# Summing and listing the presence of experts over 82 blocks instead of 128

## The chip, the core and the metric

The kernel runs on one core of a Trainium2 chip. The metric is the device time of one execution, in microseconds. TensorE (PE; its weight loads PEld) multiplies matrices into PSUM; VectorE (DVE), ScalarE (ACT) and GpSimd (POOL) work beside it; SyncE (SP) issues most DMAs, and GpSimd the indirect ones.

## The reference

A trunk of two layers on 256 frames of 1024 channels: latent attention, then sparse attention, each followed by PEER, a mixer that picks 16 of 16384 experts for each of 8 heads of a token. The change touches PEER alone:

```python
v1, i1 = lax.top_k(s1, PEER_TOPK)
v2, i2 = lax.top_k(s2, PEER_TOPK)
...
best, pos = lax.top_k(cand, PEER_TOPK)
expert = jnp.take_along_axis(cand_idx, pos, axis=-1)
gate = jax.nn.softmax(best, axis=-1)
...
    u = w_down[e_blk]
    a = jnp.einsum('td,ted->te', x_blk, u).astype(jnp.float32)
    hg = (jax.nn.gelu(a, approximate=False) * g_blk).astype(w_up.dtype)
    return jnp.einsum('te,ted->td', hg, w_up[e_blk]).astype(x_blk.dtype)
```

So each token uses 128 experts: a row of `w_down`, a gelu, a gate, and a row of `w_up`.

## The kernel before

**Blocks.** The 16384 experts form 128 blocks of 128. For the down projection the kernel doesn't gather: for each block it multiplies all 128 rows of `w_down` with all 256 tokens (`d`, 48 matmuls of 256 columns for two blocks, since every f32 operand is split in a high and a low f16 part: `hi`, `lo`, `xh`, `xl`), applies gelu and multiplies with a gate that is zero where a token doesn't use the expert. The result `A` has 128 blocks of 128 experts x 256 tokens.

**Placing.** The gates are brought into that form while the `d` matmuls run. For four tokens at a time, a group, `prepare` (lines 1369 to 1375) makes one-hot matrices `hot` and gates `gate`, and `place` multiplies them: for each token two matmuls of 128 columns into `G` (high and low part of the gate) and, behind the first of them, one into `seen` with the same weights `hot[:, 0, :, j]`. `seen` sums the gates over 128 tokens, so that a value over zero says that the expert in that row and block is used by a token of that half. VectorE and ScalarE then take `G` into `A` (lines 1393 and 1395), and the gelu of the new block with them (1566 to 1569). Two groups stand in each step of two blocks, until all 64 are done.

**Listing.** `w_up` is used in 46 dense blocks (`DENSE`), with all their rows, and for the other 82 blocks only in rows that are used. For each partition, `lists` finds which blocks hold a used expert: for both halves of the tokens (24 and, sent from fuller partitions to others by the `moved` matmuls, 16 more), for the first half alone (16) and the second alone (16). It compares `seen` with zero, forms products, weighs them with `weight16`, a falling number for each block that is zero for the dense ones, and takes 8 maxima at a time (MAX8 and MATCH_REPLACE8, lines 1417 and 1418). At its end stand the row numbers `up_at` and `act_at` (lines 1491 to 1496). Its steps are interleaved with the first steps of the up projection `y`.

**Gathering.** `A` of the 82 blocks goes to DRAM (`abuf`, line 1508, on SP's queue between the loads of dense blocks, line 222). GpSimd's indirect DMAs fetch rows of `w_up` (line 219) and of `abuf` (1527, 1532) by these lists, and TensorE multiplies them (`y`, 512 columns).

**Order.** A scheduler that simulates the program sets the order of instructions on each engine; the code adds chains on some engines (`dve`, `pe`). All matmuls but a few are recorded at line 460, all splits at 166 and 175.

Of the kernel before, what the change touches and what calls it, by code (L numbers as in the profile page):

```python
# [16 lines left out]
ALU = mybir.AluOpType  # L17
AX = mybir.AxisListType

P = 128  # L20
# [46 lines left out]
BOTH, MOSTLY = 128, 896  # L67
CHECKS = 7 * P
DENSE, HEAD = 46, 22
JB, JO, TB, ROWTAIL = 24, 16, 16, 32  # L70
BOTHS = JB + TB
LISTED = BOTHS + 2 * JO
# [257 lines left out]
def tile_trunk(ctx: ExitStack, tc: tile.TileContext, ins, out: bass.AP, short, shared):  # L330
    nc = tc.nc
# [16 lines left out]
    def oh_tile(tag, dt=F32):  # L348
        return ohp.tile([P, 4, P], dt, tag=tag, name=tag)

    def ps(name):
        return psp.tile([P, 512], F32, tag="ps", name=name)

    def py(i, name):
        if short:
            shared["banks"][i] = pyp.tile([P, 512], F32, tag=f"py{i}", name=name)
        return shared["banks"][i]
# [29 lines left out]
    if short:  # L387
        abuf = dram.tile([(NKEYS + 1 - DENSE) * P, T], F32, tag="abuf", name="abuf")
        weight16 = const.tile([P, P], F16, tag="weight16", name="weight16")
        below16 = const.tile([P, P], F16, tag="below16", name="below16")  # L390
        row = const.tile([P, 1], F32, tag="row", name="row")
        up_at = const.tile([P, LISTED], I32, tag="up_at", name="up_at")
        act_at = const.tile([P, LISTED], I32, tag="act_at", name="act_at")
        nc.gpsimd.iota(row, pattern=[[0, 1]], base=0, channel_multiplier=1, allow_small_or_imprecise_dtypes=True)
        nc.vector.tensor_scalar(below16, iota16, row, None, op0=ALU.is_gt)
        nc.vector.tensor_scalar(weight16, iota16, -1.0, float(NKEYS), op0=ALU.mult, op1=ALU.add)
        nc.vector.memset(weight16[:, :DENSE], 0.0)
        zero = arena[:, 30720 - T : 30720]
        nc.vector.memset(zero, 0.0)
        nc.sync.dma_start(abuf[(NKEYS - DENSE) * P :, :], zero)  # L400
# [33 lines left out]
    def link(engine, emit):  # L434

        with ExitStack() as order:
            if chains.get(engine) is not None:
                order.enter_context(tc.issue_after(chains[engine]))
            ins = emit()
        if engine in chains:  # L440
            chains[engine] = ins.ins
        return ins

    def pe(emit):
        return link("pe", emit)

    def dve(emit):
        return link("dve", emit)
# [10 lines left out]
    def mm(o, l, r, start, stop):  # L459
        return pe(lambda: nc.tensor.matmul(o, l, r, start=start, stop=stop, skip_group_check=True))  # L460
# [278 lines left out]
    begun = {}  # L739
# [435 lines left out]
    def peer(li):  # L1175
# [14 lines left out]
        hot = ar.ring(2, TOPK, CELLS)  # L1190
# [187 lines left out]
        def place(g4, done):  # L1378

            p = py(g4 % (3 if short else 4), f"G{g4}")  # L1380
            if short and g4 == 0:
                begun["seen"] = py(3, "seen")
            hot, gate = onehot.pop(g4)
            for j in range(4):
                for i in range(2):
                    mm(p[:, j * P : (j + 1) * P], hot[:, 0, :, j], gate[:, i, j, :], i == 0, i == 1)
                    if short and i == 0:
                        h, k = divmod(4 * g4 + j, P)
                        mm(begun["seen"][:, h * P : (h + 1) * P], hot[:, 0, :, j], gate[:, 0, j, :], k == 0, k == P - 1)
            pv = p.rearrange("p (t b) -> p b t", b=P)  # L1390
            tsl = slice(4 * g4, 4 * g4 + 4)
            if done < P:
                nc.scalar.mul(A[:, done:, tsl], pv[:, done:, :], 1.0 / GSCALE)
            if done:
                nc.vector.scalar_tensor_tensor(A[:, :done, tsl], pv[:, :done, :], 1.0 / GSCALE, A[:, :done, tsl],
                                               op0=ALU.mult, op1=ALU.mult)

        def lists():

            seen = begun.pop("seen")  # L1400
            key, got = oh_tile("V"), oh_tile("U")
            keys, e = small.tile([P, LISTED], F32, tag="keys", name="keys", bufs=1), got[:, 2, :LISTED]
            m8 = small.tile([P, 8], F32, tag="m8", name="m8", bufs=1)
            count = small.tile([P, 4], F32, tag="count", name="count", bufs=1)
            two = got[:, 0:2, :]
            dve(lambda: nc.vector.tensor_scalar(two, seen[:, : 2 * P].rearrange("p (t b) -> p t b", b=P), 0.0, None,
                            op0=ALU.is_gt))
            dve(lambda: nc.vector.tensor_tensor(key[:, 0, :], two[:, 0, :], two[:, 1, :], op=ALU.mult))
            yield
            dve(lambda: nc.vector.tensor_tensor(key[:, 1, :], two[:, 0, :], two[:, 1, :], op=ALU.is_gt))  # L1410
            dve(lambda: nc.vector.tensor_tensor(key[:, 2, :], two[:, 1, :], two[:, 0, :], op=ALU.is_gt))
            dve(lambda: nc.vector.tensor_tensor(key[:, 0:3, :], key[:, 0:3, :], weight16[:, None, :].to_broadcast([P,
                            3, P]), op=ALU.mult))
            yield

            def take(o, k):
# [23 lines left out]
            p = ps("base")  # L1440
# [27 lines left out]
            p = ps("moved")  # L1468
# [84 lines left out]
        for b0 in range(0, NKEYS, 2):  # L1553
            p = ps(f"d{b0}")
# [12 lines left out]
            if t0 > 0:  # L1567
                nc.scalar.activation(pv[:, :, :t0], pv[:, :, :t0], AF.Gelu, scale=1.0 / unit)
                dve(lambda: nc.vector.tensor_tensor(A[:, b0 : b0 + 2, :t0], A[:, b0 : b0 + 2, :t0], pv[:, :, :t0],
                                                    op=ALU.mult))  # L1570
            while groups < prepared:
                place(groups, b0 + 2)
                groups += 1
# [7 lines left out]
            if short:  # L1581
                if groups >= 32:
                    store(0, b0)
                    store(0, b0)
                if groups == 64:
                    if listing[0] is None:
                        chains["dve"] = None
                        listing[0] = lists()
                    if b0 < NKEYS - 2:
                        list_on(3)  # L1590
                    store(1, b0)
                    store(1, b0)
# [225 lines left out]
```

## Time and profile before

| | us |
|---|---|
| median of 3 runs | 1680.58 (1676.13 to 1681.88) |
| the profiled execution | 1678.09 |
| its span, first to last instruction | 1676.3 |
| placing stage of layer 0, about | 297 to 513 |
| placing stage of layer 1, about | 1150 to 1362 |
| first gather by the lists of layer 0 | 575.83 |

A group line of the profile gives line, engine, operation, output and inputs, shapes and count, then busy time and the mean duration in ns, then the idle time just before these instructions and what ended it. A line of the timeline gives start and length in us. A line of windows gives a stretch, its length, the busy time of each engine, the clock that TensorE was granted, the mean busy share of the 16 DMA engines and GB/s.

### The profile page before, as it was taken

What the parts mean: (1) busy time and instruction counts of PE and PEld (TensorE: products, weight loads), DVE (VectorE), ACT (ScalarE), POOL (GpSimd) and SP (SyncE); (2) the same over time, 40 slices, a digit from 0 to 9 for tenths busy, and PEclk for the clock granted to TensorE, in tenths of its full rate; (3) what the DMA queues carried; (4) which work ended last, traced back from release to release, by engine and by line L of the source; (5) the groups of instructions that cost most, each with busy time, mean ns of one, the idle gap of its engine ahead of it and who ended that gap; (6) DMA issues with size and microseconds to landing.
All of it is one profiled execution on the core that took longest, in us unless ns stands there. A gap on an engine that the chain in (4) does not pass through costs nothing.

```text
span 1676.3 us, 33243 instructions
## 1 busy us (share of the span) xinstructions
PE 1609.7 (96%) x12451; PEld 1163.6 (69%) x12451; DVE 1347.5 (80%) x3212; ACT 1064.2 (63%) x1865; POOL 531.3 (32%) x419
## 2 busy tenths in 40 slices
PE   9999999999999999999899999999999999999995
PEld 7678888999996443444577688888999974444432
DVE  8689999989997756666788799999989978466565
ACT  7666656888884445554568665576888854455452
POOL 2011255000000277877032022441000000788783
PEclk9999999999999999999999999999999999999998
DMA  9445656655758677777855555556547567777773
GB/s 342 157 171 173 203 179 208 209 164 179 231 184 249 243 256 250 265 259 244 298 199 172 185 184 179 202 183 218 169 154 252 181 206 271 247 262 254 271 241 132
DMA packets 139963, 361.44 MB, mean 216 GB/s; under 512 B 13712, under 2 KB 56848, under 8 KB 139792
## 3 DMA queue, kind: packets, MB, share of 16 engines
q1 hardware_dynamic: 112880, 268.51, 47.8%
q0 software_dynamic: 26624, 90.20, 16.5%
q8 instruction: 99, 1.62, 0.4%
q14 instruction: 72, 0.59, 0.1%
q10 hardware_dynamic: 288, 0.52, 0.1%
HBM read 333.35 MB, written 25.82 MB: 214 GB/s over the span
## 4 chain that ended last, share of the span: by engine, by line
PE 51%; DMA 11%; issue 11%; POOL 11%; DVE 11%; ACT 3%; SPq 2%; POOLq 0%; DVEq 0%; ACTq 0%
PE d L460 34%; DMA raw<-in_up,up_at 7%; DVE lo L175 5%; POOL raw L219 5%; PE y L460 4%; PE G L460 3%; PE pq L460 2%; POOL U L1527 2%; POOL U L1532 2%; PE seen L460 2%; ACT hi L166 2%; SPq L1508 1%; DMA raw<-in_up 1%; POOL V L1532 1%; PE qw L460 1%
## 5 line engine op out<-in xcount | busy, mean ns | idle before, releaser
L175 DVE SCALAR_TENSOR_TENSOR lo<-raw,hi 128x1024 f16<-128x1024 f32 (+2 forms) x550 | 695.5, 1275 | 217.0 <-ACT hi L166 169.6
L166 ACT ACTIVATE hi<-raw 128x1024 f16<-128x1024 f32 (+2 forms) x550 | 570.0, 1050 | 384.9 <-DMA raw<-in_up,up_at 169.1
L460 PE MATMUL d<-xh,lo 128*128 128x256 f16 x2048 | 558.5, 273 | 0.9 <-DVE lo L175 0.9
L460 PE MATMUL d<-xh,hi 128*128 128x256 f16 x2048 | 558.6, 273 | 0.0
L460 PE MATMUL d<-xl,hi 128*128 128x256 f16 x2048 | 558.5, 273 | 0.0
L460 PEld LDWEIGHTS <-hi 128*128 128x128 f16 x5016 | 489.0, 98 | 57.7 <-issue 0.9
L219 POOL DMA_INDIRECT raw<-in_up,up_at x144 | 172.1, 1195 | 612.4 <-DVE act_at L1496 566.0
L460 PEld LDWEIGHTS <-xh 128*128 128x128 f16 x1904 | 185.4, 98 | 251.2 <-issue 32.0
L460 PE MATMUL y<-lo,xh 128*128 128x512 f16 x880 | 265.2, 379 | 12.0 <-DVE lo L175 8.1
L460 PE MATMUL y<-hi,xh 128*128 128x512 f16 x880 | 264.0, 380 | 11.3 <-ACT hi L166 5.8
L460 PEld LDWEIGHTS <-lo 128*128 128x128 f16 x2508 | 245.8, 98 | 31.9 <-DVE lo L175 2.7
L460 PE MATMUL y<-hi,xl 128*128 128x512 f16 x880 | 264.4, 380 | 2.1 <-DVE xl L175 1.9
L1375 ACT ACTIVATE gate<-hot,rest 128x128 f16<-128x128 f16 x512 | 168.0, 406 | 20.6 <-DVE hot L1369 18.7
L460 PEld LDWEIGHTS <-xl 128*128 128x128 f16 x952 | 92.1, 98 | 120.9 <-DVE xl L175 7.5
L257 POOL TENSOR_TENSOR lo<-raw,hi 128x1024 f16<-128x1024 f32 x27 | 63.3, 2346 | 212.1 <-ACT hi L255 161.1
L1369 DVE TENSOR_TENSOR hot<-iota,place 128x1024 f16<-128x1024 f16 x128 | 87.7, 689 | 19.3 <-PE G L460 18.6
L460 PE MATMUL G<-gate,hot 128*128 128x128 f16 x1024 | 96.2, 219 | 2.1 <-DVE gate L1371 2.1
L460 PEld LDWEIGHTS <-hot 128*128 128x128 f16 x1536 | 92.8, 113 | 3.1 <-DVE gate L1371 2.4
L1290 POOL TENSOR_TENSOR arena<-arena 128x800 f32<-128x800 f16 x32 | 70.7, 2210 | 62.7 <-DVE arena L1287 62.7
L460 PE MATMUL seen<-gate,hot 128*128 128x128 f16 x512 | 89.1, 219 | 0.0
L1371 DVE TENSOR_TENSOR gate<-hot,gate 128x512 f16<-128x512 f16 x128 | 87.6, 687 | 0.0
L253 ACT ACTIVATE raw<-raw 128x1024 f32<-128x1024 f32 x27 | 28.6, 1057 | 88.7 <-DMA raw<-in_down 80.1
(270 smaller groups left out, 1828.2 us busy)
## 6 DMA issues: line engine op xcount, KB each, us to landing
raw<-in_down SPq DMA_DIRECT2D x256, 512.0 KB
raw<-in_up SPq DMA_DIRECT2D x92, 512.0 KB
abuf<-arena SPq DMA_DIRECT2D x80, 256.0 KB
raw<-in_peer_q SPq DMA_DIRECT2D x24, 512.0 KB
raw<-in_dsa_qk SPq DMA_DIRECT2D x16, 512.0 KB
raw<-in_mla_w_o SPq DMA_DIRECT2D x8, 512.0 KB
arena<-in_peer_q SPq DMA_DIRECT2D x8, 512.0 KB
raw<-in_dsa_v SPq DMA_DIRECT2D x8, 512.0 KB
```

The source lines that it names most:

```text
L166: return nc.scalar.copy(o, src) if unit == 1.0 else nc.scalar.mul(o, src, unit)
L175: return nc.vector.scalar_tensor_tensor(o, src, unit, hi, op0=ALU.mult, op1=ALU.subtract, accum_out=total)
L219: self.fetched = self.nc.gpsimd.indirect_dma_start(t, None, table, bass.IndirectOffsetOnAxis(ap=at, axis=0)).ins
L253: self.act(lambda: nc.scalar.mul(raw, raw, unit))
L257: nc.gpsimd.tensor_tensor(lo, raw, hi if short else hi.bitcast(F32), op=ALU.subtract)
L460: return pe(lambda: nc.tensor.matmul(o, l, r, start=start, stop=stop, skip_group_check=True))
L1290: nc.gpsimd.tensor_tensor(o.rearrange("p k c -> p c k"), same, cell[t][:, h, :, None].to_broadcast([P, CELLS, TOPK]), op=ALU.mult)
L1369: nc.vector.tensor_tensor(hot, iota4[:, None].to_broadcast([P, 2, P, 4]), place16[:, :, None, four].to_broadcast([P, 2, P, 4]), op=ALU.is_ ...
L1371: engine.tensor_tensor(gate[:, 0], hot[:, 1].rearrange("p c j -> p j c"), gate16[:, four, None].to_broadcast([P, 4, P]), op=ALU.mult)
L1375: nc.scalar.mul(gate[:, 1, j, :], hot[:, 1, :, j], rest[:, t : t + 1])
L1527: gp(lambda: nc.gpsimd.indirect_dma_start(o, None, abuf, bass.IndirectOffsetOnAxis(ap=at, axis=0)))
L1532: gp(lambda: nc.gpsimd.indirect_dma_start(t[:, 2 + h, :], None, halves, bass.IndirectOffsetOnAxis(ap=at, axis=0)))
```

## The change

`seen` is summed over the columns of the 82 blocks that may be listed (`RARE = P - DENSE`), and `lists` works on 82 columns. `weight16` is read from column 46 on, so its memset to zero for the dense blocks goes.

```diff
 DENSE, HEAD = 46, 22
+RARE = P - DENSE
@@
         nc.vector.tensor_scalar(weight16, iota16, -1.0, float(NKEYS), op0=ALU.mult, op1=ALU.add)
-        nc.vector.memset(weight16[:, :DENSE], 0.0)
@@ place
-                        mm(begun["seen"][:, h * P : (h + 1) * P], hot[:, 0, :, j], gate[:, 0, j, :], k == 0, k == P - 1)
+                        mm(begun["seen"][:, h * RARE : (h + 1) * RARE], hot[:, 0, :, j], gate[:, 0, j, DENSE:], k == 0,
+                           k == P - 1)
@@ lists
-            two = got[:, 0:2, :]
-            dve(lambda: nc.vector.tensor_scalar(two, seen[:, : 2 * P].rearrange("p (t b) -> p t b", b=P), 0.0, None,
+            two, key = got[:, 0:2, :RARE], key[:, :, :RARE]
+            dve(lambda: nc.vector.tensor_scalar(two, seen[:, : 2 * RARE].rearrange("p (t b) -> p t b", b=RARE), 0.0, None,
                             op0=ALU.is_gt))
...
-            dve(lambda: nc.vector.tensor_tensor(key[:, 0:3, :], key[:, 0:3, :], weight16[:, None, :].to_broadcast([P,
-                            3, P]), op=ALU.mult))
+            dve(lambda: nc.vector.tensor_tensor(key[:, 0:3, :], key[:, 0:3, :], weight16[:, None, DENSE:].to_broadcast([P,
+                            3, RARE]), op=ALU.mult))
```

The scheduler sees other sizes, and so some rows stand elsewhere. (In the rows below, lines of the changed kernel are one higher, and numbers behind names are those of buffers.) VectorE in the placing stage of layer 0, at the step for blocks 92 and 93; `arena<-G` is the placing of one group, `arena<-arena,d` the gelu's product, `lo` a residual of a weight block. Before:

```order
L1395 SCALAR_TENSOR_TENSOR arena<-G_5583,arena 128x92x4
L1569 TENSOR_TENSOR arena<-arena,d_5519 128x2x120
L1395 SCALAR_TENSOR_TENSOR arena<-G_5598,arena 128x92x4
L1371 TENSOR_TENSOR gate<-hot,gate_103 128x512
L175 SCALAR_TENSOR_TENSOR lo_5775,sums<-raw_5524,hi_5774 128x1024
```

And with the change:

```order
L1396 SCALAR_TENSOR_TENSOR arena<-G_5582,arena 128x92x4
L1396 SCALAR_TENSOR_TENSOR arena<-G_5597,arena 128x92x4
L1570 TENSOR_TENSOR arena<-arena,d_5518 128x2x120
L1371 TENSOR_TENSOR gate<-hot,gate_103 128x512
L176 SCALAR_TENSOR_TENSOR lo_5774,sums<-raw_5523,hi_5773 128x1024
```

The second group's product has moved ahead of the gelu's; some twenty steps of each layer have swaps of this kind, on ScalarE too.

SP's queue behind the placing stage of layer 0, where stores of `A` to `abuf` stand between loads of up-projection blocks. Before:

```order
L1508 DMA abuf<-arena 128x4x128 x8
L222 DMA raw_7441<-in_up 128x1024
L1508 DMA abuf<-arena 128x4x128
L222 DMA raw_7482<-in_up 128x1024
L1508 DMA abuf<-arena 128x4x128 x8
L222 DMA raw_7512<-in_up 128x1024
L1508 DMA abuf<-arena 128x4x128 x2
L222 DMA raw_7555<-in_up 128x1024
```

And with the change:

```order
L1509 DMA abuf<-arena 128x4x128 x6
L223 DMA raw_7440<-in_up 128x1024
L1509 DMA abuf<-arena 128x4x128
L223 DMA raw_7481<-in_up 128x1024
L1509 DMA abuf<-arena 128x4x128 x9
L223 DMA raw_7511<-in_up 128x1024
L1509 DMA abuf<-arena 128x4x128
L223 DMA raw_7554<-in_up 128x1024
```

The loads have 6, 7, 16 and 17 stores ahead of them, where they had 8, 9, 17 and 19.

VectorE at the end of the list of layer 0; `to` makes the one-hot weights of the `moved` matmuls (eight for each `to`), `keys<-moved` copies their result. Before:

```order
L1480 TENSOR_TENSOR to<-iota_105,at_7780 128x1024 x3
L175 SCALAR_TENSOR_TENSOR xl,sums<-arena,xh 128x512
L175 SCALAR_TENSOR_TENSOR lo_7927,sums<-raw_7761,hi_7926 128x1024
L175 SCALAR_TENSOR_TENSOR lo_7945,sums<-raw_7790,hi_7944 128x1024
L175 SCALAR_TENSOR_TENSOR xl,sums<-arena,xh 128x512
L175 SCALAR_TENSOR_TENSOR lo_7965,sums<-raw_7815,hi_7964 128x1024
L1486 COPY keys<-moved 128x16
L175 SCALAR_TENSOR_TENSOR lo_7986,sums<-raw_7837,hi_7985 128x1024
L175 SCALAR_TENSOR_TENSOR lo_8006,sums<-raw_7859,hi_8005 128x1024
L1487 TENSOR_SCALAR U<-keys,row 128x72
```

And with the change:

```order
L1481 TENSOR_TENSOR to<-iota_105,at_7779 128x1024 x2
L176 SCALAR_TENSOR_TENSOR xl,sums<-arena,xh 128x512
L1481 TENSOR_TENSOR to<-iota_105,at_7779 128x1024
L176 SCALAR_TENSOR_TENSOR lo_7926,sums<-raw_7760,hi_7925 128x1024
L176 SCALAR_TENSOR_TENSOR lo_7944,sums<-raw_7789,hi_7943 128x1024
L176 SCALAR_TENSOR_TENSOR xl,sums<-arena,xh 128x512
L176 SCALAR_TENSOR_TENSOR lo_7964,sums<-raw_7814,hi_7963 128x1024
L176 SCALAR_TENSOR_TENSOR lo_7985,sums<-raw_7836,hi_7984 128x1024
L176 SCALAR_TENSOR_TENSOR lo_8005,sums<-raw_7858,hi_8004 128x1024
L1487 COPY keys<-moved 128x16
L1488 TENSOR_SCALAR U<-keys,row 128x72
```

The copy has moved behind two more residuals; the steps from `U<-keys,row` on, which end with `up_at` and `act_at`, keep their place. On TensorE, counted from the same `y` matmul, the four batches of eight `moved` matmuls stood behind 1, 4, 4 and 6 more `y` matmuls; now they stand behind 5, 7, 7 and 26. The same swaps stand in layer 1.

## The prediction

> **What bounds the kernel now.** I read the page for the engines and the groups, then the table of stages, then the chain of work that ended last, then the timeline inside one piece of that chain.
>
> ```profile
> span 1676.3 us, 33243 instructions
> PE 1609.7 (96%) x12451; PEld 1163.6 (69%) x12451; DVE 1347.5 (80%) x3212; ACT 1064.2 (63%) x1865; POOL 531.3 (32%) x419
> L460 PE MATMUL seen<-gate,hot 128*128 128x128 f16 x512 | 89.1, 219 | 0.0
> ```
>
> TensorE is busy for 96% of the span, but the shares hide stages with different limits. The 512 `seen` matmuls are what the change narrows; their 219 ns each overlap, since matmuls are pipelined, so what one costs must come from the distance between starts. The stages (columns: length, then busy time and count of PE, PEld, DVE, ACT, POOL, then clock, DMA share, GB/s):
>
> ```profile
> 147.00:297.00 150.00, 150.00 (x1377) 134.54 (x1375) 142.94 (x426) 93.91 (x117) 58.66 (x38) 1.00 0.59 190
> 310.00:505.00 195.00, 195.00 (x2135) 179.21 (x2133) 181.45 (x330) 163.96 (x423) 0.00 (x0) 1.00 0.60 190
> 1146.00:1365.00 219.00, 216.87 (x2363) 198.96 (x2361) 200.41 (x370) 176.47 (x451) 0.00 (x0) 1.00 0.58 187
> 520.00:550.00 30.00, 27.72 (x148) 14.05 (x146) 23.36 (x71) 13.83 (x19) 0.00 (x0) 1.00 1.04 343
> 580.00:800.00 220.00, 210.17 (x954) 93.26 (x953) 134.59 (x264) 114.27 (x133) 173.63 (x141) 0.99 0.77 256
> ```
>
> From 310 to 505 us, and again from 1146 to 1365, TensorE does down-projection (`d`) and gate placement (`G`, `seen`) with hardly a gap, at full clock, with the DMA at 0.60 and 0.58. All 512 `seen` matmuls lie in these two stretches or at their edges. VectorE stands close behind, 181.45 of 195 us. From 520 to 550 the DMA is full (1.04). From 580 to 800 no single busy share is near full, and the waits of GpSimd tell why:
>
> ```profile
> L219 POOL DMA_INDIRECT raw<-in_up,up_at x72 | 85.0, 1181 | 307.0 <-DVE act_at L1496 283.1 <-issue 20.1 <-DVE lo L175 2.9
> POOL raw L219 <- issue: 19.8, 65, 0.3
> ```
>
> GpSimd waits 283.1 us for the list of experts (`act_at`) and then issues one indirect DMA after another, with 0.3 us of issue time between them and 2.9 us of waiting for a buffer. So the second half of a PEER layer starts when the list is ready and keeps its length: what the placing stage loses, the end loses.
>
> The chain of waits shows the placing stage at its finest (start, length, what):
>
> ```profile
> 401.63 5.24 PE d L460 x48
> 408.21 5.24 PE d L460 x48
> ```
>
> One period is 408.21 - 401.63 = 6.58 us: 48 `d` matmuls of 256 columns in 5.24 us, 109.2 ns each, and 1.34 us for two groups of placing. The timeline of TensorE in that 1.34 us:
>
> ```profile
> 400.12 0.22 PE L460 MATMUL G<-gate,hot 128*128 128x128 f16 x1
> 400.18 0.22 PE L460 MATMUL seen<-gate,hot 128*128 128x128 f16 x1
> 400.23 0.28 PE L460 MATMUL G<-gate,hot 128*128 128x128 f16 x2
> 400.35 0.22 PE L460 MATMUL seen<-gate,hot 128*128 128x128 f16 x1
> ...
> 401.41 0.22 PE L460 MATMUL G<-gate,hot 128*128 128x128 f16 x1
> 401.46 0.27 PE L460 MATMUL d<-xh,hi 128*128 128x256 f16 x1
> ```
>
> 24 matmuls of 128 columns start between 400.12 and 401.46: 55.8 ns each, 8 of them `seen`.
>
> **The narrower matmul.** 256 columns take 109.2 ns and 128 take 55.8, so a column costs (109.2 - 55.8) / 128 = 0.417 ns, and 46 fewer save 19.2 ns: a `seen` matmul would take 36.6 ns, and 512 of them save 9.8 us. That holds if the columns alone set the distance. Each matmul also has a load of 128x128 weights, and the load doesn't shrink. Its price is bounded from two sides:
>
> ```profile
> L460 PEld LDWEIGHTS <-hot 128*128 128x128 f16 x1536 | 92.8, 113 | 3.1 <-DVE gate L1371 2.4
> L460 PEld LDWEIGHTS <-hi 128*128 128x128 f16 x5016 | 489.0, 98 | 57.7 <-issue 0.9
> 564.64 0.35 PE L1475 MATMUL moved<-sent,to 128*128 128x32 f16 x8
> L1475 PE MATMUL moved<-sent,to x64: 176/176/190, 564.6 to 1416.6; 128*128 128x32 f16 x64
> ```
>
> Eight `moved` matmuls of 32 columns, each with a load of 128x128 weights that lie side by side, take 0.35 us, the last of them 0.176: (350 - 176) / 7 = 25 ns apart. So a load can follow a load after 25 ns. The weights of `seen` are `hot[:, 0, :, j]`, every fourth element, and their load lasts 113 ns against 98. If these 15 ns are occupancy, such a load needs 40 ns; if they are latency, 25; the row at 55.8 ns says no more than that it isn't over that. I take 40, the value from this operand's own row: 15.8 ns saved, 512 x 15.8 = **8.1 us**. The ends are 9.8 (columns alone) and 0 (the load fills 55.8 already). The moving operand now starts 46 elements into its row, which no row here shows; it stays within these ends. The Trainium skill's page "TensorE: Matmul & The Clock Gate" puts a weight load, in its section "LDWEIGHTS (loading the stationary operand)", at the number of columns divided by 1.2, in ns; for 128 columns this would be 107 ns, a load would be the bound already, and by it the change would save nothing. The starts 25 and 55.8 ns apart speak against it here, so I give it no more than the rival below.
>
> **What is late next: VectorE.** Eight `seen` matmuls stand in a period, so it falls from 6.58 to 6.58 - 8 x 0.0158 = 6.45 us (6.43 by columns alone). VectorE's work in a period grows with the blocks already done:
>
> ```profile
> 335.83:342.41 6.58, 6.58 (x74) 6.05 (x73) 5.72 (x13) 5.52 (x16) 0.00 (x0) 1.00 0.55 167
> 480.59:487.17 6.58, 6.58 (x74) 6.04 (x73) 6.45 (x13) 5.32 (x15) 0.00 (x0) 1.00 0.64 202
> 487.17:493.75 6.58, 6.58 (x74) 6.05 (x73) 6.49 (x13) 5.32 (x15) 0.00 (x0) 1.00 0.51 159
> 493.75:500.33 6.58, 6.58 (x74) 6.04 (x73) 6.52 (x13) 5.31 (x15) 0.00 (x0) 1.00 0.66 199
> ```
>
> Only the last two reach over 6.45, by 0.04 and 0.07 us. That gives back 0.1 us in each layer, **0.2 us**. ScalarE has 5.3 to 5.5 us of work in a period, and the DMA 0.60 of the stage, so both follow. The swaps of line 1395 with 1569 on VectorE, and of the same tiles' work on ScalarE, keep the work of a period; I cost them at nothing, covered by VectorE's idle 0.1 to 0.9 us, and the rival on VectorE prices the loss of that cover.
>
> **The lists.** These instructions shrink from 128 to 82 columns (min, median and max of the row with a form of 50 columns too, in ns):
>
> ```profile
> L1234 DVE MAX8 arena<-arena x96: 213/295/297, 112.8 to 1112.2; 128x8 f32<-128x128 f32 x64, 128x8 f32<-128x50 f32 x32
> L1412 DVE TENSOR_TENSOR V<-V,weight x2: 557/558/560, 516.1 to 1364.8; 128x384 f32<-128x384 f32 x2
> L1406 DVE TENSOR_SCALAR U<-seen x2: 415/416/416, 513.9 to 1362.6; 128x256 f32<-128x256 f32 x2
> ```
>
> A column costs (295 - 213) / 78 = 1.05 ns, so 46 columns 48 ns. In both layers there are 22 maxima, 22 replacements, 2 last maxima and 10 products, 56 x 48 ns = 2.7 us, and 138 columns of line 1412 and 92 of line 1406, twice: 0.5 us. Together 3.2 us, 1.6 a layer. Much of it is hidden, since VectorE then waits for weight blocks that the full DMA brings:
>
> ```profile
> 540.86 1.23 DVE L175 SCALAR_TENSOR_TENSOR lo<-raw,hi 128x1024 f16<-128x1024 f32 x1 [0.78 <-ACT hi L166]
> 545.30 1.23 DVE L175 SCALAR_TENSOR_TENSOR lo<-raw,hi 128x1024 f16<-128x1024 f32 x1 [2.00 <-ACT hi L166]
> 523.08 8.04 SPq L1508 DMA_DIRECT2D abuf<-arena  x8
> ```
>
> 2.78 us of waits stand there in layer 0. On SP's queue the up-projection blocks now stand one or two stores earlier, at 8.04 / 8 = 1.0 us a store, so these waits may shrink by 1 to 2 us; but the same bytes go through a full DMA. The stores, which end later in the queue, are read by the gathers only after 575 us. The gain of this part lies between 0 and 1.6 + 2 us a layer; I take 0.5, nearer to the lower end since the DMA's bytes are unchanged: **1.0 us** in all. The removed memset is one of 78 ns at 2.9 us, before TensorE's first weights, and costs nothing either way:
>
> ```profile
> L397 DVE MEMSET weight<- x1: 78/78/78, 2.9 to 2.9; 128x23 uint32 x1
> ```
>
> **The sum.** -8.1 + 0.2 - 1.0 = -8.9 us. The profiled execution took 1678.1 us (span 1676.3), which gives 1669.2; the median of the three runs, 1680.6, lies 2.5 above it, and I forecast the median: **1671.7 us**, 0.5% less.
>
> **Rivals.** (A) The weight load bounds the placing matmuls: 55.8 ns stay, whatever the columns. For it: the load of `hot` is the slowest of the f16 loads, and no row shows it faster than 55.8 ns apart. Against it: the column price fits 128 and 256 columns with almost nothing left over (55.8 - 128 x 0.417 = 2.4 ns), which a load as the bound would not. Time: 1680.6 less 1.0 for the lists, about 1680. The Trainium skill's page "TensorE: Matmul & The Clock Gate", section "Back-to-back issue gap", has about 81 ns for sustained pairs of load and matmul at 128 columns; here they stand 55.8 apart, so it doesn't hold in this stage. Chance 0.12.
>
> (B) VectorE becomes the bound earlier than its busy time says.
>
> ```profile
> DVE hot L1369 <- PE G L460: 9.5, 18, 0.6
> 441.11:447.69 6.58, 6.58 (x74) 6.05 (x73) 6.17 (x13) 5.38 (x16) 0.00 (x0) 1.00 0.62 197
> ```
>
> In the stretch from 297 to 507 us it waits 9.5 us for placing to free a buffer, 0.3 us in each of 32 periods. If that wait stays in the last ten periods of a layer, VectorE needs 6.47 to 6.82 us there, 0.2 over 6.45 on average: 10 x 0.2 x 2 = 4 us lost, about 1676. Against it: TensorE itself frees those buffers, and sooner. Chance 0.10.
>
> (C) Slower: the list comes later. The last eight `moved` matmuls now stand 20 `y` matmuls later in TensorE's order, and the copy of their result, ahead of the list's last five steps on VectorE, waits for them.
>
> ```profile
> 567.30 0.37 PE L1475 MATMUL moved<-sent,to 128*128 128x32 f16 x8 [0.33 <-DVE to L1480]
> 549.89 10.40 PE y L460 x48
> 571.82 0.18 DVE L1486 COPY keys<-moved 128x16 f32<-128x16 f32 x1
> 571.91 1.22 DVE L175 SCALAR_TENSOR_TENSOR lo<-raw,hi 128x1024 f16<-128x1024 f32 x1
> 574.69 0.20 DVE L1491 TENSOR_SCALAR up_at<-U 128x72 int32<-128x72 f32 x1
> ```
>
> Before, `moved` ended at 567.67 and the copy ran at 571.82, 4.15 us later. A `y` matmul takes 10.40 / 48 = 0.217 us, so 20 of them 4.3 us; the copy itself moves back by two residuals of a block, 2 x 1.22 = 2.4 us. 4.15 - 4.3 + 2.4 = 2.2 us of slack remain. Past it, each microsecond that TensorE waits for a block among those matmuls delays the gathers, and with them the end. It takes 2.2 + 8.9 / 2 = 6.7 us of such waits in each layer to cancel the gain, and 2.5 us more to be 0.3% slower: 1686. Between 520 and 550 us TensorE waits 2.3 us in all. Chance 0.06.
>
> That the change doesn't do what it says is out: all 512 `seen` rows of the new order are 128x82.
>
> **How the numbers follow.** The forecast has 0.72, with a range of its own from 1667 (columns alone and 2 us a layer from the lists: -9.8 + 0.2 - 4.0 = -13.6) to 1675 (nothing from the lists, -7.9, and half of the 5.7 us between the runs of before). The whole range, 1665 to 1678, takes in B and nearly all of the ends' sum (-9.8 + 0.2 - 7.2 = -16.8 us, 1663.8), and leaves out A and C. Within 0.3% (5.0 us) is about what a measurement here can't tell from no change. Faster by more: 0.72 less 0.03 for the low end of the forecast, plus 0.05 of B, 0.74. Within: A 0.12, half of B 0.05, 0.03 of the forecast and 0.01 of C, 0.21. Slower: 0.05.
>
> **What would show it.** In the new profile the period of the placing stage should be 6.43 to 6.46 us, and a `seen` matmul should be followed after 37 to 40 ns; at 55.8, A holds. VectorE's wait for placing should fall, not stay at 9.5 us. The list (`up_at`) should be ready some 4 to 6 us earlier in layer 0 (574.69 before). GpSimd should stay without waits behind it. A wait of the `keys` copy for `moved` would be C. The prediction is wrong if the placing stage shrinks and the gathers don't move.

## The result, and the profile after

| | before | after |
|---|---|---|
| median, us (runs) | 1680.85 (11) | 1670.07 (11) |
| lowest to highest, us | 1676.13 to 1683.0 | 1661.94 to 1676.26 |
| the profiled execution, us | 1678.09 | 1667.09 |

The ratio is 0.9942, with a 95% interval from 0.9922 to 0.9963; the medians lie 10.8 us, or 0.6%, apart. (Ratios here and below are taken over all runs of both kernels, so they can stand up to 0.002 from the quotient of two medians.) Forecast were 1671.7 us, within 1665 to 1678.

From the page of the changed kernel, first the span and the busy times, then two groups (busy time, mean ns of one, idle before them):

```profile
span 1665.3 us, 33241 instructions
PE 1604.2 (96%) x12451; PEld 1156.3 (69%) x12451; DVE 1342.9 (81%) x3211; ACT 1061.9 (64%) x1865; POOL 529.2 (32%) x419
L460 PE MATMUL seen<-gate,hot 128*128 128x82 f16 x512 | 79.3, 200 | 0.0
L460 PEld LDWEIGHTS <-hot 128*128 128x128 f16 x1536 | 84.2, 113 | 3.1 <-DVE gate L1371 2.4
```

One `seen` matmul lasts 200 ns where it lasted 219. That is no measure of the gain: most of its duration lies beside the next matmuls. The chain of waits (start, length, what) gives the period, and the timeline of TensorE the distances:

```profile
391.67 5.24 PE d L460 x48
398.10 5.24 PE d L460 x48
...
430.23 5.24 PE d L460 x48
```

```profile
396.75 0.22 PE L460 MATMUL G<-gate,hot 128*128 128x128 f16 x1
396.80 0.20 PE L460 MATMUL seen<-gate,hot 128*128 128x82 f16 x1
396.84 0.28 PE L460 MATMUL G<-gate,hot 128*128 128x128 f16 x2
396.95 0.20 PE L460 MATMUL seen<-gate,hot 128*128 128x82 f16 x1
...
397.88 0.22 PE L460 MATMUL G<-gate,hot 128*128 128x128 f16 x1
397.93 0.27 PE L460 MATMUL d<-xh,hi 128*128 128x256 f16 x1
```

From the first of these three `d` groups to the last are six periods: (430.23 - 391.67) / 6 = 6.427 us, against 6.58. Eight `seen` matmuls in a period have lost 0.153 us, 19.1 ns each, and columns alone would give 46 x 0.417 = 19.2. From a `seen` to the next `G` it is 396.84 - 396.80, 36 ns where the trace is read to the nanosecond, against 55.8. The Trainium skill's page "TensorE: Matmul & The Clock Gate", section "Wait — 56ns, not 53.3ns?", puts the distance of starts at N / 2.4 + 2.5 ns, from which I estimate 36.7 for 82 columns; the trace agrees, with 36 ns here and 55.8 - 19.1 = 36.7 by the period.

The windows of the same kernel (length, then busy time and count of PE, PEld, DVE, ACT, POOL, then clock, DMA share, GB/s): the placing stage, its last two full periods, and the stage behind it, in which the list is made:

```profile
310.00:505.00 195.00, 195.00 (x2189) 178.85 (x2187) 182.57 (x334) 165.49 (x426) 0.00 (x0) 1.00 0.60 192
481.64:488.07 6.43, 6.43 (x75) 5.90 (x73) 6.40 (x12) 5.29 (x16) 0.00 (x0) 1.00 0.53 163
488.07:494.50 6.43, 6.43 (x74) 5.88 (x73) 6.43 (x12) 5.30 (x16) 0.00 (x0) 1.00 0.69 206
514.00:544.00 30.00, 27.31 (x144) 13.75 (x142) 20.71 (x63) 11.93 (x17) 0.00 (x0) 1.00 1.05 334
```

VectorE is now full in the last periods (6.40 and 6.43 of 6.43 us), and yet the period stays at 6.43. The waits (sum, count, longest) say the same of what it waits for, and that GpSimd's indirect DMAs behind the list are still bound by their issue:

```profile
DVE hot L1369 <- PE G L460: 14.6, 41, 0.4
POOL raw L220 <- issue: 39.2, 129, 0.3
```

Where the list is made, the timeline of VectorE shows longer waits (in brackets) than before, and then its last steps:

```profile
533.73 1.23 DVE L176 SCALAR_TENSOR_TENSOR lo<-raw,hi 128x1024 f16<-128x1024 f32 x1 [0.32 <-ACT hi L167]
540.56 1.23 DVE L176 SCALAR_TENSOR_TENSOR lo<-raw,hi 128x1024 f16<-128x1024 f32 x1 [4.49 <-ACT hi L167]
543.49 1.22 DVE L176 SCALAR_TENSOR_TENSOR lo<-raw,hi 128x1024 f16<-128x1024 f32 x1 [1.20 <-ACT hi L167]
...
569.80 0.17 DVE L1487 COPY keys<-moved 128x16 f32<-128x16 f32 x1
...
570.50 0.20 DVE L1492 TENSOR_SCALAR up_at<-U 128x72 int32<-128x72 f32 x1
```

6.0 us of waits for weight blocks stand there, where 2.8 were shown before. That it is the blocks shows on ScalarE, whose split `hi` VectorE waits for; it waits for the load itself:

```profile
539.47 1.06 ACT L167 ACTIVATE hi<-raw 128x1024 f16<-128x1024 f32 x1 [4.73 <-DMA raw<-in_up]
```

Where the time of the two profiled executions went, from the starts of instructions in the traces (us):

| stage | before | after | difference |
|---|---|---|---|
| start to the first `seen` of layer 0 | 308.06 | 306.83 | -1.23 |
| layer 0, first to last `seen` | 205.15 | 200.26 | -4.89 |
| layer 0, last `seen` to `up_at` | 61.48 | 63.41 | +1.93 |
| layer 0, first gather to last `y` | 233.61 | 230.66 | -2.95 |
| layer 1, first to last `seen` | 205.15 | 201.93 | -3.22 |
| layer 1, last `seen` to `up_at` | 61.87 | 62.41 | +0.54 |
| layer 1, first gather to last `y` | 232.44 | 232.41 | -0.03 |

The rest of the 11.0 us, -1.1, lies between and behind these stages. The stages of placing got shorter, those of the list longer. (Layer 1's placing lost less, 3.2 us, because a stretch at half clock fell into it; the last section has more on it.) The row of layer 0's gathers can't be read from one pair of executions: in other profiles below, of the changed kernel too, it is between 230 and 241 us.

### The profile page after: what moved, and what is told of

Its sections match the earlier page's. It is cut to its first block, busy times and chain, and to the rows that moved or that the text cites. A ratio compares the mean times of both kernels' runs of the same rounds, so it can differ in the third digit from the quotient of the medians.

```text
span 1665.3 us, 33241 instructions
## 1 busy us (share of the span) xinstructions
PE 1604.2 (96%) x12451; PEld 1156.3 (69%) x12451; DVE 1342.9 (81%) x3211; ACT 1061.9 (64%) x1865; POOL 529.2 (32%) x419
## 4 chain that ended last, share of the span: by engine, by line
PE 54%; DMA 11%; POOL 11%; issue 10%; DVE 10%; ACT 3%; SPq 2%; POOLq 0%; DVEq 0%; ACTq 0%
PE d L460 35%; DMA raw<-in_up,up_at 6%; DVE lo L176 5%; POOL raw L220 4%; PE y L460 4%; PE G L460 3%; POOL U L1528 2%; PE pq L460 2%; POOL U L1533 2%; DMA V<-abuf,act_at 2%; ACT hi L167 2%; PE q L460 2%; DMA raw<-in_up 1%; SPq L1509 1%; PE seen L460 1%
## 5 line engine op out<-in xcount | busy, mean ns | idle before, releaser
L1369 DVE TENSOR_TENSOR hot<-iota,place 128x1024 f16<-128x1024 f16 x128 | 87.5, 688 | 15.3 <-PE G L460 14.6
L460 PE MATMUL G<-gate,hot 128*128 128x128 f16 x1024 | 86.4, 220 | 2.1 <-DVE gate L1371 2.1
L460 PEld LDWEIGHTS <-hot 128*128 128x128 f16 x1536 | 84.2, 113 | 3.1 <-DVE gate L1371 2.4
L460 PE MATMUL seen<-gate,hot 128*128 128x82 f16 x512 | 79.3, 200 | 0.0
```

The lines of the kernel that those rows point to most:

```text
L1369: nc.vector.tensor_tensor(hot, iota4[:, None].to_broadcast([P, 2, P, 4]), place16[:, :, None, four].to_broadcast([P, 2, P, 4]), op=ALU.is_ ...
```

## The experiments

All ratios are to runs of the kernel before on the same chip. My theory after the result: the narrower `seen` carries the gain, at its price by columns; the shorter lists carry nothing, since their work lies beside the DMA's transfers of weight blocks. The rivals: the lists carry a part; the load of the strided weights, not the columns, is what sets the new distance.

**The changed kernel again**, to know the scatter.

> The changed kernel once more, as the yardstick of this series. Theory (columns): the 512 seen matmuls start 36 ns apart where it was 55.8, the period of the placing stage is 6.43 us, the time is 9 to 12 us under the kernel before (ratio 0.993 to 0.995). Rival (a lucky set of runs): the gain of 10.8 us doesn't come back, ratio 0.997 or more. A second profile also shows whether the half-clock stretches of TensorE (eight of 3.4 us in the first profile, three in the one of before) belong to the change or differ from run to run.

1671.68 us (8 runs) against 1683.48 (25): 0.9935, interval 0.9913 to 0.9958. Layer 0's gather stage is 236.5 us here, 6 more than above, in a kernel with the same instructions.

**The narrower matmul alone.** The first of 128 tokens still sums all columns, which clears them, and the lists work on 128.

```diff
+                        lo = 0 if k == 0 else DENSE
-                        mm(begun["seen"][:, h * P : (h + 1) * P], hot[:, 0, :, j], gate[:, 0, j, :], k == 0, k == P - 1)
+                        mm(begun["seen"][:, h * P + lo : (h + 1) * P], hot[:, 0, :, j], gate[:, 0, j, lo:], k == 0, k == P - 1)
```

> The kernel before with one edit: all seen matmuls but the first of each half sum 82 columns; lists still work on 128. Theory (columns): the whole gain of TensorE is here, 508 x 19.3 ns = 9.8 us, ratio 0.993 to 0.995, as the full change. Rival (lists): the shorter list carries a part of it, and this kernel gains 6 us or less, ratio 0.9965 or more.

1673.56 us, 0.9946 (0.9924 to 0.9967): 9.1 us faster, nearly the whole gain. The period is that of the changed kernel, 392.33 - 385.90 = 6.43 us:

```profile
385.90 5.24 PE d L460 x48
392.33 5.24 PE d L460 x48
```

The list is ready 62.7 us behind the last `seen` in both layers, later than before (61.5 and 61.9), and that without any change of the lists.

**The shorter lists alone.** `seen` sums 128 columns again, and the lists read 82 of them.

```diff
...
-            dve(lambda: nc.vector.tensor_scalar(two, seen[:, : 2 * RARE].rearrange("p (t b) -> p t b", b=RARE), 0.0, None,
+            dve(lambda: nc.vector.tensor_scalar(two, seen[:, : 2 * P].rearrange("p (t b) -> p t b", b=P)[:, :, DENSE:], 0.0, None,
```

> The changed kernel with one edit undone: seen sums all 128 columns again, lists work on 82 of them. Theory (columns): the 3.2 us of work taken from VectorE turn into waits for weight blocks, period 6.58 us, ratio 0.999 to 1.001. Rival (lists): 3 us or more are gained, ratio 0.998 or less, and the list is ready 1.5 us or more sooner after the last seen matmul than the 61.5 us of before.

1679.39 us, 0.9983 (0.9963 to 1.0004): not clear of nothing. So it ran once more, with a longer series:

> The kernel with the shorter lists alone (placing matmuls of 128 columns, period 6.58 us), which stood at -2.8 us against before, within an interval of -6.2 to +0.7 us. If the saved list work is hidden, as the stage from the last seen to the list says (61.8 and 61.3 us, against 61.5 and 61.9 before), the total is that of before within 2 us. If the shorter lists are worth the 3.2 us of VectorE work they remove, it is 3 us less.

1677.31 us (12 runs) against 1678.41 (23): 1.0004 (0.9985 to 1.0023). The lists alone carry nothing that can be measured. In the chain of waits of this kernel the period is the old one, 396.90 - 390.32 = 6.58 us:

```profile
390.32 5.24 PE d L460 x48
396.90 5.24 PE d L460 x48
```

The list stands 61.8 and 62.2 us behind the last `seen` (61.8 and 61.3 in the first series), as before, and VectorE idles 8.6 to 9.4 us in between instead of 7.3 to 7.7. The 1.6 us of work that each list loses became 0.9 to 1.9 us more of waiting.

**Two matmuls of 41 columns.** The same columns, but twice as many loads of `hot`.

```diff
-                        mm(begun["seen"][:, h * RARE : (h + 1) * RARE], hot[:, 0, :, j], gate[:, 0, j, DENSE:], k == 0,
-                           k == P - 1)
+                        for c in (0, RARE // 2):
+                            mm(begun["seen"][:, h * RARE + c : h * RARE + c + RARE // 2], hot[:, 0, :, j],
+                               gate[:, 0, j, DENSE + c : DENSE + c + RARE // 2], k == 0, k == P - 1)
```

> The changed kernel with each seen matmul split in two of 41 columns, each with its own weight load: 1024 of them, the same sum. It measures the load of strided weights. If a load may follow a load after 25 ns, as for weights that lie side by side, the pair takes 50 ns where one of 82 takes 36: 14 x 512 = 7 us slower than the changed kernel. If a load of hot needs 36 ns or so (just hidden now), the pair takes 72 ns, 18 us slower, above the kernel before. If it needs 40 ns the first profile's 36 ns would not have been seen.

1689.77 us, 1.0044 (1.0026 to 1.0062), 18 us over the changed kernel on this chip. Two rows of its chain of waits, and three of its timeline:

```profile
397.02 5.24 PE d L460 x48
403.70 5.24 PE d L460 x48
```

```profile
402.10 0.22 PE L460 MATMUL G<-gate,hot 128*128 128x128 f16 x1
402.15 0.22 PE L460 MATMUL seen<-gate,hot 128*128 128x41 f16 x2
402.21 0.28 PE L460 MATMUL G<-gate,hot 128*128 128x128 f16 x2
```

The period is 6.68 us, so eight more matmuls cost 0.253 us, 32 ns each; a pair takes 36.7 + 31.6 = 68.3 ns, or 34 for each, where the columns of one (41 x 0.417 + 2.4) make 19.5. This 34 is a mean: read to the nanosecond, the second of a pair starts 28 ns behind the first, the next `G` 35 ns behind the second, and the `G` after that 61 ns later, where it is 57 in the changed kernel. So something beside the columns costs time here. It isn't a floor of every matmul, since `moved` follows at 25. I take it for the load of weights that lie four elements apart, but that isn't shown: no run changed the stride alone. The mean stands between the 25 and the 40 ns of the prediction, and just under the 36.7 that 82 columns take. What refutes the rival is the distance at 82 columns itself, which the columns explain. By this price my estimate is that a narrower `seen` would stop paying at (34 - 2.4) / 0.417, about 76 columns.

**A wider matmul**, of 164 columns, to price a column in the other direction. It sums 82 columns of the gate's low part beside those of the high part, and the lists read the latter alone.

```diff
+                        mm(begun["seen"][:, 2 * h * RARE : 2 * (h + 1) * RARE].rearrange("p (i b) -> p i b", i=2), hot[:, 0, :, j],
+                           gate[:, :, j, DENSE:], k == 0, k == P - 1)
...
```

> The changed kernel with a seen matmul of 164 columns: beside the 82 of the gate's high part it sums 82 of its low part, which nobody reads. Theory (columns): a column costs 0.417 ns on TensorE, and nothing else bounds the stage, so a seen matmul takes 164 x 0.417 + 2.4 = 70.8 ns, the period is 6.43 + 8 x 0.0342 = 6.70 us, and the time is 512 x 34.2 ns = 17.5 us above the changed kernel, about 1.004 of the kernel before. Rival (something else than TensorE, VectorE above all, sets a part of the period of 6.43 us): less than 14 us above it.

1690.33 us, 1.0072 (1.0052 to 1.0091). Its stages are as forecast, with a period of 399.66 - 392.96 = 6.70 us and 209.0 us from first to last `seen` in both layers (8.7 over those of the changed kernel, 17.4 in both):

```profile
392.96 5.24 PE d L460 x48
399.66 5.24 PE d L460 x48
```

The total missed what I expected, 1.004. The changed kernel had not run on that chip, so both ran together on a third one:

> The changed kernel beside the next one, on the same chip, to settle the last comparison, which the kernel before on another chip had to carry. Theory (columns): ratio 0.992 to 0.996.

> The kernel with 164 columns again. Theory (columns): 17.5 us above the changed kernel on the same chip, within the scatter of 3 us. Rival (something beside TensorE's columns costs time in it): 23 us, as the first runs had by way of the kernel before.

The changed kernel took 1670.03 us, 0.9941 (0.9906 to 0.9976), and that of 164 columns 1686.81, 1.0037 (1.0014 to 1.006): 16.8 us apart, where 82 columns x 0.417 ns x 512 make 17.5. The price of a column holds; the higher first total I put down to the scatter between series.

**What makes the list wait: half of the stores left out.** In the kernel with the narrower matmul alone, and in the changed one, the stores of `A` for the second half of the tokens, which stand between the loads of weight blocks, are left out. A second piece of the edit, not printed below, fills that half of `abuf` with another matrix during the placing stage of layer 0, so that the gathers fetch as many rows as before, with other values.

```diff
-        stored = [DENSE, DENSE]
+        stored = [DENSE, NKEYS if short else DENSE]
...
```

> As the kernel with the narrow seen and lists of 128, but the stores of the second half of the tokens to DRAM are left out, so that the gathers of that half fetch rows of another matrix, written there ahead of layer 0's placing. It takes half of the stores from the full DMA of the list stage. Theory (the DMA hides the list's work): VectorE's idle time between the last seen and the list, 8.1 us in each layer with all stores, falls to 4 us or less, and the list comes 3 us or more sooner than 62.7 us behind the last seen. Rival (the ring of weight blocks or TensorE's pace hides it): it stays at 61 us or more.

> The same half of the stores left out of the changed kernel, lists of 82. Theory (the DMA hides the list's work): now the 1.6 us a layer that the shorter instructions save come through: from the last seen to the list 1.2 to 1.8 us less than in the run before it with lists of 128. Rival: less than 0.5 us between the two.

Each stands on one execution. With lists of 128 columns the list is ready 57.1 us behind the last `seen` in both layers, with 82 columns 56.8. Against the 62.7 of the narrower matmul alone that is 5.6 us sooner: these stores do set when the list comes, by their bytes or by their places ahead of the loads in SP's queue, which these runs don't part. But I had also expected that, with the DMA relieved, the shorter lists would show their 1.6 us; they show 0.3. VectorE idles 4.5 us with the short lists against 3.2, and now for TensorE, a wait that the kernel with all its stores doesn't have (lists of 128 columns, then of 82, both layers together):

```profile
DVE count L1444 <- PE base L1442: 3.9, 2, 1.9
DVE count L1444 <- PE base L1442: 5.2, 2, 2.6
```

So that part of the theory fell: two covers lie over the list's work, the blocks and, behind them, TensorE's pace.

**More list work.** Each take of maxima does two more on VectorE, 22 of 245 ns or 5.4 us in each layer.

```diff
+                for _ in range(2):
+                    dve(lambda: nc.vector.max(m8, k))
```

> The changed kernel with two more MAX8 of 82 columns at each of the 11 places in a layer where a list takes eight maxima; their result is overwritten. That is 22 x 0.25 = 5.5 us more of list work on VectorE in a layer. Theory (the list's work is hidden, by weight blocks that arrive late): VectorE's idle time behind the last seen, 9.5 to 11 us in a layer, falls by about 5 us, and the list comes less than 1.5 us later than the 62 to 64 us of the changed kernel. Rival (VectorE's work sets the list): it comes 4 us or more later, and the kernel is some 8 us or more slower.

One run came at 1679.84 us, which I had not expected: the list was no later (62.5 us in both layers), but the gather stages took 241 and 236 us. Timed:

> The changed kernel with two more maxima at each take (5.5 us more VectorE work in each layer's list), which came at 1679.8 us in one run, with the list no later than in the changed kernel but a gather stage 5 to 11 us longer. If list work is hidden and that longer stage was the scatter of one run, the median stands within 3 us of the changed kernel (0.994 of before). If the longer list costs time in a place that the stage up to the list does not show, it stays at 8 to 11 us over the changed kernel, about the time of before.

1671.54 us (12 runs), 0.9956 (0.9938 to 0.9974). That is 0.0015 over the changed kernel's 0.9941, 2.5 us, within the intervals, for 11 us of work. The list is ready at 63.1 and 62.8 us, and VectorE's idle, 9.1 to 11.2 us in the three profiles of the changed kernel, falls to 6.1 and 6.4. So list work is hidden, nearly all of it, and the slow gathers were the scatter of one run.

## Why the prediction was right, point by point

**The narrower matmul** was the right term, and too small: 8.1 us forecast, (6.58 - 6.427) x 32 x 2 = 9.8 measured, its end by columns alone. The step that was off is "I take 40, the value from this operand's own row". It read the 15 ns by which the load lasts longer as time that the next load has to wait. At 82 columns no such wait shows; two matmuls of 41 columns stand 34 ns apart in the mean, 9 over the 25 of `moved` and not 15, and 34 lies under 36.7, so the load sets nothing here. **Rival A** is refuted.

**VectorE** was to give back 0.2 us. It gave back nothing: it is full for two periods, and they stay at 6.43 us. The step that was wrong is to set 6.52 us of busy time against the period, for records on VectorE that follow at once overlap. Two rows of the changed kernel, of which the second starts 0.08 us before the first ends:

```profile
487.51 0.69 DVE L1369 TENSOR_TENSOR hot<-iota,place 128x1024 f16<-128x1024 f16 x1
488.12 1.22 DVE L176 SCALAR_TENSOR_TENSOR lo<-raw,hi 128x1024 f16<-128x1024 f32 x1
```

The durations of the 11 instructions that start in such a late period sum to 7.2 us in both kernels, and they fit into 6.58 us (from 493.75, before) and into 6.43 (from 488.07, after). **Rival B** is refuted: the wait for placing fell to 14.6 us, and in the stretch from 297 to 507 us, where the prediction read 9.5, to 6.6. Two rows, the whole span of the kernel before and that stretch of the changed one:

```profile
DVE hot L1369 <- PE G L460: 18.6, 35, 0.6
DVE hot L1369 <- PE G L460: 6.6, 19, 0.4
```

**The lists** were to gain 0.5 us a layer, "between 0 and 1.6 + 2 us". Alone they gain nothing (1.0004, and 0.9983 in the first series), so the lower end was the value: their work lies beside waits, and the loads that stand earlier in SP's queue didn't shorten these. What I had left out is that this stage gets longer when the placing stage gets shorter. From last `seen` to `up_at`, over all profiles but the two with stores left out, 12 values of each kind:

| period of the placing stage | list stage, us | mean |
|---|---|---|
| 6.58 to 6.70 us (six profiles, lists of 82 columns in all but one) | 61.3 to 62.2 | 61.7 |
| 6.43 us (six profiles, one with lists of 128, two with more work) | 61.8 to 63.9 | 62.8 |

So about 1.1 of the 4.9 us are paid back in each layer, whatever the lists' length. They lie in the first part of the list: from the start of `base` to that of `up_at` it takes 24.8 to 25.1 us in every one of these profiles. The runs with half of the stores show that the stores hold this stage up; that the faster placing leaves less time to bring blocks ahead fits the longer waits, but was not shown by itself. A rival stands open: the scheduler's order of ScalarE's splits and of SP's stores in this stage differs from kernel to kernel too, and no run changes the period with this order held. By these terms 2 x (4.9 - 1.1) = 7.6 us are gained, less some 0.8 for the stretch at half clock in layer 1's placing, which costs 1.7 us and stands in four of the six profiles with the short period and in one of the other six. Measured were 9.7, 10.9 and 9.9 us in three series (ratios 0.9942, 0.9935, 0.9941 of about 1680), and 9.1 with the narrower matmul alone. Some 2 to 4 us of it I can't place; the gather stages scatter by more.

**The sum**, -8.9, was so near to -10.8 with a seen term 1.7 too small, a list term whose gain didn't come and a loss in that stage that wasn't in it. The mechanism of the main term held; that the total came so near is in part luck. **Rival C** did not happen: the last `moved` matmuls ended 1.4 us ahead of the copy (569.80), where 2.2 us of slack were worked out.

```profile
568.02 0.35 PE L1476 MATMUL moved<-sent,to 128*128 128x32 f16 x8
```

The signs that were named came true: 36 ns behind a `seen` (just under the 37 to 40 forecast), 6.43 us for the period, no new wait of GpSimd, and the list of layer 0 at 570.50, 4.2 us sooner. The last is right in sum only: -1.2 us ahead of the stage, -4.9 in it, +1.9 behind it. Two readings were off and bore nothing: the memset at 2.9 us doesn't stand ahead of TensorE's first weights, since a load of `iota` starts at 2.28 us, and these loads of `iota`, 128 ns in the mean, are longer f16 loads than those of `hot`.

## What to carry to other kernels

Price a narrower matmul by the distance of starts, two widths of the same kernel side by side, and the weight load by a row of such loads packed closely; a load's longer duration said little here of the distance that it forces. Before counting work that is saved on an engine, look whether it waits for something in that stretch: here 1.6 us less work a list, and even 5.4 us more, hardly moved the end. A stage that follows a shortened one can give a part back (here 1.1 of 4.9 us), perhaps since there is less time to bring things ahead during the first one.

## What was not expected of the hardware

TensorE runs at half clock for 3.4 us at a time, or twice that, behind waits. Windows of the changed kernel, ahead of, in and behind one such stretch:

```profile
543.10:546.50 3.40, 1.08 (x6) 0.51 (x6) 2.94 (x11) 2.88 (x4) 0.00 (x0) 1.00 1.03 418
546.50:549.90 3.40, 3.40 (x9) 1.21 (x8) 3.23 (x12) 2.07 (x3) 0.00 (x0) 0.50 1.02 405
549.90:553.30 3.40, 3.40 (x17) 1.58 (x16) 3.37 (x10) 2.30 (x3) 0.00 (x0) 1.00 1.02 399
```

The granted clock is 0.50, and 9 matmuls stand in it where 17 do in the next 3.4 us. Ahead of it TensorE had waited 3.45 us for VectorE; before the change the same wait was 1.33 us, and no such stretch followed (timelines, after and before):

```profile
545.42 0.16 PE L1442 MATMUL base<-n,below 128*128 128x1 f16 x1 [3.45 <-DVE n L1436]
...
1149.49 0.25 PE L460 MATMUL G<-gate,hot 128*128 128x128 f16 x1 [2.12 <-DVE gate L1371]
```

```profile
549.73 0.16 PE L1441 MATMUL base<-n,below 128*128 128x1 f16 x1 [1.33 <-DVE n L1435]
...
1156.66 0.24 PE L460 MATMUL G<-gate,hot 128*128 128x128 f16 x1 [2.13 <-DVE gate L1371]
```

A wait doesn't decide it alone. In layer 1 TensorE waits 2.1 us ahead of the first `G` in both kernels; in the profile above a stretch at half clock follows and costs the placing stage 1.7 us, before and in the third profile of the changed kernel none does. Nor does it belong to the change: with the shorter lists alone, at a period of 6.58 us, one profile has it too (206.8 us from first to last `seen` in layer 1, where it was 205.15). The Trainium skill's page "TensorE: Matmul & The Clock Gate", section "What's actually happening", tells of a free-running window of 3.4 us by whose load the clock is set, and the length of these stretches agrees. They cost the list nothing here: from `base` to `up_at` the three profiles of the changed kernel take 25.1 us, five times with such a stretch and once without, and it took 25.0 before, without one.
